# Norm sums as products with a matrix of ones, factors on all partitions, and pooling by doubling additions

## The chip, the cores and the metric

The kernel runs on one core of a Trainium2 chip. The metric is the device time of one execution in microseconds (us); the median of three runs of the kernel before is 1076.26 us (1076.07 to 1076.46).

## The reference

One decoder layer for two request groups that share all weights: one sequence of 256 new tokens, and 8 sequences with 4 new tokens each, 288 tokens in all. The model width is 2048; everything is fp32.

```python
h = rmsnorm(x, norm1_g)                                   # first norm
a, gate, z = split(h @ w_in + b_in, [1024, 1024, 1024])
u = a * sigmoid(gate)                                     # conv heads
c = silu(layernorm(depthwise_causal_conv(u_ext, conv_w, conv_b), ln_g, ln_b))
d = window_mean(z_ext, windows=(2, 4, 8, 16)) - z         # one window per 256 channels
p = grouped_matmul(d, pool_w) * pool_scale
x = x + concat([c, p]) @ w_out
f = square(relu(rmsnorm(x, norm2_g) @ w_ff1))             # 2048 -> 8192
x = x + f @ w_ff2
y = rmsnorm(x, norm_f)
```

`rmsnorm` needs for each token the sum of squares over 2048 channels; `layernorm` needs the mean and the sum of squares over 1024 channels. The window mean of the first tokens of a sequence divides by fewer elements than the window. The last inputs of the convolution and of the pooling are outputs too.

## The kernel before

Channels lie on the 128 partitions and the 288 tokens along the free axis, so that a [128 x 288] tile is one eighth of 1024 channels. Weights come from HBM as blocks of 512 KB (`wr`, 128 x 1024, six buffers). For fp32 accuracy each operand is split in a high part in fp32r and a low part, which is what the high part misses. `split` (L288) makes `whi` by an ACT copy (L293) and `wlo` by a subtraction (L294) on POOL or, for the second half of the w_out blocks, on DVE; each has four buffers. `product` (L297) is then three matmuls: high x high (L300), high x low (L301), low x high (L302). A `gemm` (L304) runs such products over the k-tiles for the two 128-column halves of a block pair, into two of four PSUM banks `ac`. After each gemm DVE evicts the banks.

The stages, in order: the first two groups of w_in columns on raw blocks (L367 to L400); five more conv groups and four pool groups in the order of `SEQUENCE`, with the small `pool_w` products (`mix_group`) between; the half of w_out that takes the pooled channels (eight gemms, loop at L548, operands `ph`, `pl`); the half that takes the convolved channels (L560, operands `mh`, `ml`); ff1 and ff2 in four chunks; the final norm. Matmuls of neighbouring gemms may be interleaved: a scheduler orders each engine's instructions from the program's priorities, and every engine then works through its own list strictly in that order. DVE also has a long low-priority list: the taps of the convolution (L443), and from ff1 on the products of some ff2 rows (`own_products`, L604).

What the change touches:

- **First norm.** `square` sums squares of x on all partitions into `tot` (L398). `token_sum` (L232) multiplies 96 tokens at a time by a column of ones, so that `total` is [96 x 3], tokens on partitions. `rsqrt_rows` (L266) takes ACT's square root, improves it with five small DVE instructions on [96 x 3] (L275 to L279), and spreads the factor over all partitions by three products with an identity into the bank `pr` (L285). DVE copies it to `rb` (L404), and every eviction of a w_in bank multiplies by `rb`.
- **LayerNorm of the convolution.** POOL adds up the eight tiles `c` in `sum_c`. `norm_begin` (L518), called after the third w_out gemm, multiplies `sum_c` by `avg`, a matrix of 1/1024 (L521, fp32), subtracts the mean from each tile (L524) and adds up squares in `ssc`. `norm_end` (L533), called after the fifth, does `token_sum` into `pt`, `rsqrt_rows` into `pr`, and for each tile: `n` = c times `pr` (DVE, L540), `cc` = Silu (ACT, L543), `mh` = copy (ACT, L544), `ml` = the rest (DVE, L545). `load_table` (L216) is an ACT instruction that brings in the table of the next function.
- **Pooling.** `pool_group` (L452) forms the window sum of a tile with `tensor_reduce` over a strided view (L471 for the sequence, L472 for the 8 x 4 sample tokens), for the window of 16 in two steps (L469 first). `rise` corrects the first tokens, and L474 and L476 divide by the window and subtract z. ACT copies to `dh` (L478), DVE makes `dl` (L479).

`column_sum` (L244) and `rsqrt_wide` (L249) already serve the norm ahead of ff1: two matmuls with a matrix of ones in fp32r put the sum on all partitions (`pss`, L247), and the same refinement runs on [128 x 288].

## Time and profile before

| | us |
|---|---|
| median of three runs | 1076.26 |
| the profiled execution | 1076.56 |
| its span | 1074.7 |
| PE busy | 1062.6 |
| DVE busy | 942.6 |
| POOL busy | 752.3 |
| ACT busy | 478.8 |

The span is the time from the first to the last instruction that the profiler saw; the profiled execution is 1.9 us longer than it. PE is TensorE, DVE VectorE, ACT ScalarE, POOL GpSimd and SP the engine that issues the DMAs; PEld is PE's loading of weights. PEclk is the share of TensorE's clock that was granted. A row such as `214.43 0.43 ACT L544 CAST mh<-cc` gives start, duration, engine, line, operation, and output and input by their names in the program. What stands behind the arrow in square brackets or after the bar is the idle time ahead of it and what ended it. An fp32 product (not fp32r) leaves two records.

### The profile page before, as it was taken

Reading aid. Unit: us, or ns where it says so; the run is one execution under the profiler, and the core shown is the slowest. Engines: PE = TensorE matmul, PEld = TensorE weight load, DVE = VectorE, ACT = ScalarE, POOL = GpSimd, SP = SyncE. Lnnn points to the kernel's source line nnn. Section 1 sums busy time; section 2 is a strip of 40 time slices with the busy share of each in tenths; the row PEclk is TensorE's granted clock in tenths of the full one; section 3 lists DMA queues with packets and bytes.
Section 4 is the critical chain, followed back from the end, with each engine's and each line's share of the span. In section 5 each row is a group of like instructions: output and inputs, shape, how many; then the busy total and the mean of one; then the engine's idle time right before and its main releaser. Section 6 shows DMA issues by size and latency. Waiting matters only on the chain.

```text
span 1074.7 us, 21425 instructions
## 1 busy us (share of the span) xinstructions
PE 1062.6 (99%) x8163; PEld 1061.3 (99%) x8163; DVE 942.6 (88%) x2117; ACT 478.8 (45%) x650; POOL 752.3 (70%) x400
## 2 busy tenths in 40 slices
PE   8999999999999999999999999999999999999996
PEld 8999999999999999999999999999999999999996
DVE  7799999687399999999999999999999999999553
ACT  7544455576445433334444333444433334444441
POOL 0899888503889987788888877888878788850001
PEclk9999999999999999999999999999999999999998
DMA  9655567565687777777797777777778888885522
GB/s 334 225 187 177 179 192 216 173 200 165 216 287 249 259 250 250 250 248 251 239 276 247 251 246 250 247 253 248 242 241 281 277 268 270 276 260 174 170 97 89
DMA packets 74663, 247.38 MB, mean 230 GB/s; under 512 B 7872, under 2 KB 17088, under 8 KB 74560
## 3 DMA queue, kind: packets, MB, share of 16 engines
q1 hardware_dynamic: 74128, 245.36, 70.0%
q8 instruction: 64, 1.05, 0.4%
q10 hardware_dynamic: 432, 0.64, 0.2%
q14 instruction: 39, 0.32, 0.1%
HBM read 241.25 MB, written 4.72 MB: 229 GB/s over the span
## 4 chain that ended last, share of the span: by engine, by line
PE 98%; DMA 0%; DVE 0%; ACT 0%; SPq 0%; issue 0%; DVEq 0%
PE ac L300 32%; PE ac L301 32%; PE ac L302 32%; PE ac L390 1%; PE cv L390 1%; DMA xT<-in_xT 0%; DVE xT L693 0%; PE pr L285 0%; ACT hh L376 0%; ACT uz L360 0%; PE pf L235 0%; ACT whi L383 0%; PE m L300 0%; PE m L302 0%; PE m L301 0%
## 5 line engine op out<-in xcount | busy, mean ns | idle before, releaser
L294 POOL TENSOR_TENSOR wlo<-wr,whi 128x1024 fp32r<-128x1024 f32 x282 | 675.7, 2404 | 177.9 <-ACT whi L293 177.1
L621 DVE SCALAR_TENSOR_TENSOR own<-uz,own 128x288 f32<-128x288 f32 x1397 | 605.1, 519 | 0.0
L293 ACT CAST whi<-wr 128x1024 fp32r<-128x1024 f32 x330 | 345.2, 1047 | 537.0 <-PE ac L301 485.1
L302 PE MATMUL ac<-ah,wlo 128*128 128x288 f32 x1024 | 298.1, 291 | 0.0
L301 PE MATMUL ac<-al,whi 128*128 128x288 f32 x1024 | 298.1, 291 | 0.0
L300 PE MATMUL ac<-ah,whi 128*128 128x288 f32 x1024 | 298.1, 291 | 0.0
L300 PE MATMUL ac<-fh,whi 128*128 128x288 f32 x1013 | 295.0, 291 | 0.0
L302 PE MATMUL ac<-fh,wlo 128*128 128x288 f32 x1013 | 294.9, 291 | 0.0
L301 PE MATMUL ac<-fl,whi 128*128 128x288 f32 x1013 | 294.9, 291 | 0.0
L302 PEld LDWEIGHTS ac<-ah,wlo 128*128 128x128 f32 x1024 | 191.7, 187 | 0.0
L300 PEld LDWEIGHTS ac<-ah,whi 128*128 128x128 f32 x1024 | 191.7, 187 | 0.0
L301 PEld LDWEIGHTS ac<-al,whi 128*128 128x128 f32 x1024 | 191.7, 187 | 0.0
L300 PEld LDWEIGHTS ac<-fh,whi 128*128 128x128 f32 x1013 | 189.6, 187 | 0.0
L301 PEld LDWEIGHTS ac<-fl,whi 128*128 128x128 f32 x1013 | 189.6, 187 | 0.0
L302 PEld LDWEIGHTS ac<-fh,wlo 128*128 128x128 f32 x1013 | 189.6, 187 | 0.0
L443 DVE SCALAR_TENSOR_TENSOR pc<-uz,vec,pc 128x256 f32<-128x256 f32 x232 | 99.2, 485 | 5.3 <-ACT pc L432 3.5
L301 PE MATMUL ac<-hl,whi 128*128 128x288 f32 x320 | 92.1, 291 | 0.0
L300 PE MATMUL ac<-hh,whi 128*128 128x288 f32 x320 | 92.0, 291 | 0.0
L302 PE MATMUL ac<-hh,wlo 128*128 128x288 f32 x320 | 87.3, 291 | 0.0
L294 DVE TENSOR_TENSOR wlo<-wr,whi 128x1024 fp32r<-128x1024 f32 x48 | 58.7, 1224 | 29.9 <-ACT whi L293 29.8
L693 POOL TENSOR_TENSOR xT<-xT,rg 128x576 f32<-128x576 f32 x2 | 2.8, 1408 | 99.4 <-ACT rg L698 99.4
L648 POOL TENSOR_TENSOR fl<-f,fh 128x288 fp32r<-128x288 f32 x64 | 53.5, 836 | 15.3 <-ACT fh L647 15.3
(174 smaller groups left out, 1056.0 us busy)
## 6 DMA issues: line engine op xcount, KB each, us to landing
wr<-in_w SPq DMA_DIRECT2D x336, 512.0 KB, 4.6
uz<-fd SPq DMA_DIRECT2D x96, 576.0 KB, 5.8
uz<-in_w SPq DMA_DIRECT2D x24, 128.0 KB, 6.8
out_u_out<-uz SPq DMA_DIRECT2D x1, 1208.0 KB, 8.8
xT<-in_xT SPq DMA_DIRECT2D x2, 576.0 KB, 8.1
uz<-in_hist_c SPq DMA_DIRECT2D x1, 1088.0 KB, 12.0
wr<-in_w SPq DMA_DIRECT2D x4, 256.0 KB, 5.4
xT<-in_xT SPq DMA_DIRECT2D x3, 288.0 KB, 6.1
```

Source lines behind the costliest of these rows:

```text
L293: nc.scalar.copy(hi[:, a:b, :], raw[:, a:b, :])
L294: eng.tensor_tensor(lo[:, a:b, :], raw[:, a:b, :], hi[:, a:b, :].bitcast(F32), op=ALU.subtract)
L300: nc.tensor.matmul(b, wh, xh, start=first, stop=False)
L301: nc.tensor.matmul(b, wh, xl, start=False, stop=False)
L302: nc.tensor.matmul(b, wl, xh, start=False, stop=last)
L390: nc.tensor.matmul(first_banks[m][:, :T], lhs(w, k, m), pair[k][x], start=c == 0 and k == 0 and w is hi and x == 0, stop=c == 7 and k == 1 ...
L443: nc.vector.scalar_tensor_tensor(out=dst, in0=u_all[:, i, w : w + SEQ], scalar=cw[i][:, w : w + 1], in1=pc[i], op0=ALU.mult, op1=ALU.add)
L621: nc.vector.scalar_tensor_tensor(out=to, in0=at[:, r, :], scalar=by, in1=to, op0=ALU.mult, op1=ALU.add)
L648: nc.gpsimd.tensor_tensor(fl, f, f32(fh), op=ALU.subtract)
L693: eng.tensor_tensor(xk, xk, by[:, None, :T].to_broadcast([P, n, T]), op=ALU.mult)
```

## The change

The first norm and the LayerNorm take `column_sum` and `rsqrt_wide` in place of `token_sum` and `rsqrt_rows`: `total` and `pt` become full banks, each filled by two fp32r products; their factors are computed on [128 x 288] and are on all partitions at once, so that the `pr` products and the copy to `rb` go. The mean is a column sum too, with the division put into the instruction that subtracts it. To split a row in `th` and `tl` an ACT copy and a DVE subtraction are added (`parts`; ff1's norm keeps POOL for both). Pooling adds shifted copies, with shift 1, 2, 4, 8: each step is an ACT copy of the running sum to PSUM and one DVE addition of that copy and the shifted sum. Lines of the new kernel stand 4 to 6 further down than in the old one.

```diff
+PAD = 32
...
+    gap = const.tile([P, PAD], F32, name="gap")
+    nc.gpsimd.memset(gap, 0.0)
...
-    avg = const.tile([P, P], F32, name="avg")
-    nc.vector.memset(avg, 1.0 / DC)
...
-    def parts(t):
+    def parts(t, hi=nc.scalar.copy, lo=nc.vector):
 
         th, tl = (tmpp.tile([P, T], F32R, name=nm(n), tag="tmp", bufs=6) for n in ("th", "tl"))
-        nc.gpsimd.tensor_copy(th, t)
-        nc.gpsimd.tensor_tensor(tl, t, f32(th), op=ALU.subtract)
+        hi(th, t)
+        lo.tensor_tensor(tl, t, f32(th), op=ALU.subtract)
         return th, tl
...
-    def rsqrt_wide(bank, out, scale):
+    def rsqrt_wide(bank, out, scale, after=None):
...
         nc.scalar.activation(s1, b, AF.Sqrt, bias=eps[:, 0:1], scale=scale)
+        if after is not None:
+            load_table(after, s1[:, 0:1])
...
-    total = ms("total", 8)
+    total = ms("total")
...
-                    token_sum(total, rows[0])
+                    column_sum(total, ones_r, hilo)
...
                     nc.vector.tensor_tensor(rows[0], squares[:, 0, 0], squares[:, 0, 1], op=ALU.add)
+                    hilo = parts(rows[0])
...
-    nc.vector.tensor_copy(rb, rsqrt_rows(total, 1.0 / D, AF.Sigmoid)[:, :T])
+    rsqrt_wide(total, rb, 1.0 / D, AF.Sigmoid)
...
-            b = ms("d")[:, :T]
-            s, step, n = z, 1, w
-            if w > 8:
-                s, step, n = tmp("s", ZL, "s", 2), 4, w // 4
-                nc.vector.tensor_reduce(s[:, 3:ZL], windows(z[:, 0 : ZL - 3], (1, ZL - 3), (1, 4)), axis=AX.X, op=ALU.add)
-            at = PH - step * (n - 1)
-            nc.vector.tensor_reduce(b[:, 0:SEQ], windows(s[:, at:], (1, SEQ), (step, n)), axis=AX.X, op=ALU.add)
-            nc.vector.tensor_reduce(samples(b[:, SEQ:T], NS), windows(s[:, ZO + at :], (ZS, NB), (1, NS), (step, n)), axis=AX.X, op=ALU.add)
+            s, r = ms("d"), z
+            for step in WINDOWS[: g + 1]:
+                n = ZL - step + 1
+                nc.scalar.copy(s[:, 0:n], r[:, 0:n])
+                to = s if step == w else tmp("r", ZL, "r", 2)
+                nc.vector.tensor_tensor(to[:, 0:n], s[:, 0:n], r[:, step // 2 : step // 2 + n], op=ALU.add)
+                r = to
+            at = PH - (w - 1)
...
-        nc.tensor.matmul(pmean[:, :T], avg, sum_c, start=True, stop=True)
+        column_sum(pmean, ones_r, parts(sum_c))
...
-            nc.vector.tensor_tensor(cs[i], cs[i], pmean[:, :T], op=ALU.subtract)
+            nc.vector.scalar_tensor_tensor(out=cs[i], in0=pmean[:, :T], scalar=-1.0 / DC, in1=cs[i], op0=ALU.mult, op1=ALU.add)
...
-        pt = ms("pt", 8)
-        token_sum(pt, ssc)
-        rl = rsqrt_rows(pt, 1.0 / DC, AF.Silu)
+        rl = ms("pt")
+        column_sum(rl, ones_r, parts(ssc))
+        rsqrt_wide(rl, rl[:, :T], 1.0 / DC, AF.Silu)
...
-    ss2 = parts(ss2)
+    ss2 = parts(ss2, nc.gpsimd.tensor_copy, nc.gpsimd)
```

The scheduler also orders three places anew. The first two are the LayerNorm, late in the pooled half of w_out. This is DVE's list there before (`wlo68`, `wlo69` are low parts of weights, `ac41` to `ac43` banks of the pooled half, `pt1` the sum, `st2` the factor's small tile, `pr2` the spread factor):

```order
L275 TENSOR_SCALAR pt1_2661<-pt1_2661 96x3
L276 RECIPROCAL st2_2665<-st2_2665 96x3
L277 TENSOR_TENSOR pt1_2661<-pt1_2661,st2_2665 96x3
L552 TENSOR_TENSOR xT_88<-xT_88,ac41_2804 128x288
L278 SCALAR_TENSOR_TENSOR st2_2665<-st2_2665,pt1_2661 96x3
L552 TENSOR_TENSOR xT_88<-xT_88,ac42_2805 128x288
L279 RECIPROCAL st2_2665<-st2_2665 96x3
L294 TENSOR_TENSOR wlo68_2927<-wr68_2920,whi68_2926 128x1024
L540 TENSOR_TENSOR n1_2677<-c1_540,pr2_2673 128x288
L294 TENSOR_TENSOR wlo69_2987<-wr69_2982,whi69_2986 128x1024
L540 TENSOR_TENSOR n2_2685<-c2_543,pr2_2673 128x288
L545 TENSOR_TENSOR ml1_2680<-cc1_2681,mh1_2679 128x288
```

And after (`s3`, `s4` are the wide temporaries, and the factor ends up in `pt1` itself):

```order
L258 TENSOR_SCALAR pt1_2697<-pt1_2697 128x288
L259 RECIPROCAL s4_2705<-s3_2704 128x288
L298 TENSOR_TENSOR wlo69_3023<-wr69_3018,whi69_3022 128x1024
L260 TENSOR_TENSOR pt1_2697<-pt1_2697,s4_2705 128x288
L558 TENSOR_TENSOR xT_88<-xT_88,ac43_2904 128x288
L558 TENSOR_TENSOR xT_88<-xT_88,ac44_2905 128x288
L261 SCALAR_TENSOR_TENSOR s4_2705<-s3_2704,pt1_2697 128x288
L298 TENSOR_TENSOR wlo70_3027<-wr70_3020,whi70_3026 128x1024
L262 RECIPROCAL pt1_2697<-s4_2705 128x288
L546 TENSOR_TENSOR n1_2713<-c1_539,pt1_2697 128x288
L546 TENSOR_TENSOR n2_2721<-c2_542,pt1_2697 128x288
```

Between the start of the factor and the first `n` one weight split and two evictions (`ac41`, `ac42`) stood before. Now two weight splits stand there and the evictions of `ac43` and `ac44`, the banks of the last pooled gemm. PE's list moved with it: before, the three `pt` products stood ahead of 34 matmuls of the pooled half, then the three `pr` products, and then 23 matmuls until the first `mh`; now the second `pt` product has 32 matmuls behind it, the last of the pooled half, and then comes `mh1`.

ACT's list at the same place before:

```order
L272 ACTIVATE st2_2665<-pt1_2661,eps_125 96x3
L218 ACT_TABLE_LOAD
L218 ACTIVATE few_124<-st2_2665 96x1
L293 CAST whi68_2926<-wr68_2920 128x1024
L293 CAST whi69_2986<-wr69_2982 128x1024
L543 ACTIVATE cc1_2681<-n1_2677,vec_87 128x288
L544 CAST mh1_2679<-cc1_2681 128x288
```

And after:

```order
L242 CAST th3_2698<-ssc1_2538 128x288
L297 CAST whi68_2962<-wr68_2956 128x1024
L255 ACTIVATE s3_2704<-pt1_2697,eps_125 128x288
L220 ACT_TABLE_LOAD
L220 ACTIVATE few_124<-s3_2704 128x1
L297 CAST whi69_3022<-wr69_3018 128x1024
L297 CAST whi70_3026<-wr70_3020 128x1024
L549 ACTIVATE cc1_2717<-n1_2713,vec_87 128x288
L549 ACTIVATE cc2_2725<-n2_2721,vec_87 128x288
L550 CAST mh1_2715<-cc1_2717 128x288
```

`whi69` and `whi70` both stand ahead of the first Silu now, and the second Silu ahead of the first copy `mh1`.

The third place is PE in the conv groups, at the seam of two gemms. Before, with the last reader of `whi25` 28 rows above the first row shown here:

```order
L300 MATMUL ac12_1282<-hh9_331,whi27_1191 128x288
L301 MATMUL ac12_1282<-hl9_332,whi27_1191 128x288
L300 MATMUL ac13_1447<-hh1_178,whi29_1383 128x288
L301 MATMUL ac13_1447<-hl1_179,whi29_1383 128x288
L300 MATMUL ac14_1448<-hh1_178,whi29_1383 128x288
```

And after:

```order
L304 MATMUL ac12_1281<-hh4_234,whi25_1178 128x288
L305 MATMUL ac12_1281<-hl4_235,whi25_1178 128x288
L306 MATMUL ac12_1281<-hh4_234,wlo25_1179 128x288
L304 MATMUL ac11_1280<-hh5_255,whi26_1182 128x288
L305 MATMUL ac11_1280<-hl5_256,whi26_1182 128x288
L304 MATMUL ac12_1281<-hh5_255,whi26_1182 128x288
L305 MATMUL ac12_1281<-hl5_256,whi26_1182 128x288
L304 MATMUL ac13_1446<-hh1_178,whi29_1382 128x288
```

`whi29` takes the buffer of `whi25` (four buffers, in turn). Its first product came 30 matmuls behind the last reader of that buffer, and now comes 6 behind.

## The prediction

> **What bounds the kernel now.** I read the chain that ended last first, then the waits of PE.

> ```profile
> PE 98%; DMA 0%; DVE 0%; ACT 0%; SPq 0%; issue 0%; DVEq 0%
> ```
> ```profile
> core 0 of [0], span 1074.7 us
> PE ac L390 <- ACT whi L383: 1.7, 1, 1.7
> PE warm L223 <- DVE ones L207: 1.1, 1, 1.1
> PE pr L285 <- DVE st L279: 0.5, 1, 0.5
> ```

> The chain is PE for 98% of the span, and these three waits are all that PE has; two fall in the first 9 us and one in the final norm. So PE issues without a stop, and only two things can move the time: fewer PE cycles, or a new PE wait. Work on DVE, ACT or POOL counts only where PE would wait for it. A change of 0.2% (2.15 us, hence 1074.1 to 1078.4) is about what a measurement here can tell from none.

> **PE's products.** The rows of PE's timeline at the sum `pt`, the spread `pr`, the mean `pmean`, and the products that will take their place (`pss`, in ff1's norm), with the groups of the like products of the first norm:

> ```profile
> L285 PE MATMUL pr<-ident,st 96*128 96x96 f32 x18 | 2.5, 274 | 0.5 <-DVE st L279 0.5
> L235 PE MATMUL total<-ones,tot 128*96 128x1 f32 x6 | 0.6, 214 | 0.0
> ```
> ```profile
> 207.47 0.59 PE L235 MATMUL pt<-ones,ssc 128*96 128x1 f32 x6
> 207.92 0.38 PE L300 MATMUL ac<-ph,whi 128*128 128x288 f32 x1
> 208.14 0.30 PE L301 MATMUL ac<-pl,whi 128*128 128x288 f32 x1
> ...
> 212.43 0.80 PE L285 MATMUL pr<-ident,st 96*128 96x96 f32 x6
> 213.02 0.38 PE L301 MATMUL ac<-pl,whi 128*128 128x288 f32 x1
> 213.23 0.29 PE L302 MATMUL ac<-ph,wlo 128*128 128x288 f32 x1
> ```
> ```profile
> 196.58 0.65 PE L521 MATMUL pmean<-sum_c,avg 128*128 128x288 f32 x2
> 196.85 0.51 PE L301 MATMUL ac<-pl,whi 128*128 128x288 f32 x1
> 197.20 0.29 PE L302 MATMUL ac<-ph,wlo 128*128 128x288 f32 x1
> ```
> ```profile
> 276.67 0.30 PE L247 MATMUL pss<-tl,ones_r 128*128 128x288 f32 x1
> 276.81 0.29 PE L302 MATMUL ac<-ah,wlo 128*128 128x288 f32 x1
> ```

> Matmuls overlap, so starts are subtracted, not durations added. Ordinary matmuls start 0.13 apart (156 in 20 us in the row of windows under Pooling). From `pt` at 207.47 to the second matmul behind it at 208.14 is 0.67; less one regular 0.13 the sum costs 0.54. `pr` costs 213.23 - 212.43 - 0.13 = 0.67. `pmean` costs 197.20 - 196.58 - 0.13 = 0.49. The first norm's `total` has the same six records of the same mean length, and its `pr` is among the 18 records of one mean, so 0.54 and 0.67 again. Removed: 2 x 0.54 + 2 x 0.67 + 0.49 = 2.91 us. Added: six fp32r products that cost 276.81 - 276.67 = 0.14 each, 0.84. **Net -2.07 us**, sure as far as PE goes.

> **First norm.** The factor now needs the wide chain (rows below): from the second `total` product 0.3 + 0.5 + 0.37 + 1.94 + 0.9 + 2.0 = 6 us, some 3 us more than the small one. PE works meanwhile on the third conv group in the two free `ac` banks, 96 matmuls or 12.5 us long, and `rb` is first needed by the evictions that free banks for the group after. Cost taken: nothing; if the cover were too short, at most those 3 us.

> **Pooling.** The grouped rows of the reductions, and PE, DVE and ACT in the busiest stretch:

> ```profile
> L471 DVE TENSOR_REDUCE d<-uz 128x256 f32<-128x2048 f32 (+2 forms) x6 | 8.4, 1406 | 0.0
> L469 DVE TENSOR_REDUCE s<-uz 128x420 f32<-128x1680 f32 x2 | 3.8, 1894 | 0.0
> L471 DVE TENSOR_REDUCE d<-s 128x256 f32<-128x1024 f32 x2 | 3.8, 1888 | 0.0
> ```
> ```profile
> 120.00:140.00 20.00, 20.00 (x156) 20.00 (x155) 20.00 (x51) 11.02 (x20) 14.39 (x7) 1.00 0.59 187
> ```

> The last row gives busy us of PE, PEld, DVE, ACT and POOL. DVE is full there, yet PE does not wait: it is filled with low-priority taps. The change takes 16 us of reductions (and the small sample ones) from DVE and gives it 2 x (1 + 2 + 3 + 4) = 20 additions of some 422 columns. A 288-column DVE instruction has a pitch of 0.37 (rows below), so an estimate of 0.37 x 422 / 288 = 0.54 each, 11 us: DVE gains 5 us or more, off PE's path. ACT, 11 of 20 busy, gets 20 copies; from the 0.43 of the `mh` copy an estimate of 0.63 each, 12.6 us. Per tile the chain becomes longer for all windows: for 16, 4 x (0.63 + 0.54) = 4.7 where L469 and L471 took 3.8. The queues that matter are ACT's: behind these copies, each of which waits for DVE, stand casts of weights that PE will need. Bounds: 0 (PE's operands still early; no gain is possible where PE does not wait) to 1 us; I take **+0.3**, since the chain grows by about a microsecond per tile and PE has a whole gemm between a pool group and its mix.

> A side effect of the new order is nearer to PE: `whi29` is used 6 matmuls behind the last reader of its buffer. The reader starts at 0 and ends after 0.29; the cast takes 1.05 (the `whi` row below); PE arrives after 6 x 0.13 = 0.78. 1.34 + 0.03 - 0.78 = **+0.6**; between 0.4 and 0.9.

> SP's queue has ff2's eight loads for `turned` two weight blocks earlier; those blocks are read a whole gemm later. Nothing.

> **The LayerNorm decides.** First the wide chain as it runs in ff1's norm, where it has cover, on DVE and on ACT:

> ```profile
> 278.64 0.47 DVE L254 TENSOR_SCALAR pss<-pss 128x288 f32<-128x288 f32 x1 [3.05 <-ACT s L253]
> 279.01 1.94 DVE L255 RECIPROCAL s<-s 128x288 f32<-128x288 f32 x1
> ...
> 281.98 1.95 DVE L258 RECIPROCAL r<-s 128x288 f32<-128x288 f32 x1
> ```
> ```profile
> 278.10 0.50 ACT L253 ACTIVATE s<-pss,eps 128x288 f32<-128x288 f32 x1
> ```

> Then the place itself in the kernel before, ACT, DVE and PE:

> ```profile
> 208.37 1.28 ACT L218 ACT_TABLE_LOAD   x1
> 209.67 0.20 ACT L218 ACTIVATE few<-st 96x1 f32<-96x1 f32 x1
> ...
> 212.42 1.05 ACT L293 CAST whi<-wr 128x1024 fp32r<-128x1024 f32 x1 [1.61 <-issue]
> 213.77 0.63 ACT L543 ACTIVATE cc<-n,vec 128x288 f32<-128x288 f32 x1 [0.30 <-DVE n L540]
> 214.43 0.43 ACT L544 CAST mh<-cc 128x288 fp32r<-128x288 f32 x1
> ```
> ```profile
> 213.28 0.46 DVE L540 TENSOR_TENSOR n<-c,pr 128x288 f32<-128x288 f32 x1 [1.21 <-PE pr L285]
> 213.65 1.22 DVE L294 TENSOR_TENSOR wlo<-wr,whi 128x1024 fp32r<-128x1024 f32 x1
> 214.78 0.45 DVE L540 TENSOR_TENSOR n<-c,pr 128x288 f32<-128x288 f32 x1
> 215.15 0.46 DVE L545 TENSOR_TENSOR ml<-cc,mh 128x288 fp32r<-128x288 f32 x1
> ```
> ```profile
> 216.09 0.42 PE L300 MATMUL ac<-mh,whi 128*128 128x288 f32 x2
> ```

> Before, `mh` is ready at 214.43 + 0.43 = 214.86 and PE arrives at 216.09: 1.2 us to spare, with 8.6 us of matmuls between `pt` and `mh`. After, the order leaves 32 matmuls behind the second `pt` product: with it 0.14 + 32 x 0.13 = 4.3 us, and PE's next instruction needs `mh1`. From that product's start: it ends at 0.30; ACT's root from 0.34 to 0.84. ACT then loads the table (1.28), does `few` (0.2) and casts `whi69` (1.05): 3.4. DVE meanwhile does L254 (pitch 279.01 - 278.64 = 0.37) and the reciprocal (1.94): 3.2. Then its list runs in order: `wlo69` (pitch 214.78 - 213.65 = 1.13) from 3.4 to 4.5; L256, two evictions and L257 at 0.37 each (pitch 215.15 - 214.78), to 6.0; `wlo70` 1.13, to 7.1; the second reciprocal 1.95 + 0.1, to 9.2; `n1` until the Silu may start, 213.77 - 213.28 = 0.49, to 9.7; two Silu of about 0.6, to 10.9; `mh1` 0.43, to 11.3. PE is free at 4.3: a **wait of 7.0 us**. Bounds: 6.5 (Silus pipelined, hand-overs free) to 7.8 (each of some eight hand-overs 0.1 dearer). After it, a k-step (n, Silu, copy, rest) takes under 1.1 us of ACT and 0.74 of DVE, PE's 12 matmuls for it in four banks 1.56: no further wait.

> **The clock after the wait.** The kernel's end, PE's last row and the windows behind it (PEclk is the third number from the end):

> ```profile
> 1065.26 0.83 PE L285 MATMUL again<-ident,st 96*128 96x96 f32 x6
> ```
> ```profile
> 1066.00:1068.00 2.00, 0.09 (x1) 0.00 (x0) 2.00 (x4) 0.40 (x1) 1.40 (x2) 1.00 0.51 183
> 1069.00:1070.00 1.00, 0.00 (x0) 0.00 (x0) 0.53 (x1) 0.00 (x0) 0.38 (x1) 0.65 1.05 414
> ```

> PE ends at 1066.09. The mean clock of 1069 to 1070 is 0.65, which is 0.3 us at 1 and the rest at 0.5: the clock halved at 1069.3, 3.2 us after the last matmul. The 1.7 us wait near the start is shorter than that; 7 us is longer. So PE resumes at half clock. How long, no row of before shows. If the rise takes as long as the fall, 3.2 us give 1.6 us' worth of work: **+1.6**. Bounds 0 to 3.2.

> [...]

> **Sum.** -2.07 + 0.3 + 0.6 + 7.0 + 1.6 = +7.4 on the profiled 1076.56, or 1084.0; that execution lies 0.3 above the median of the runs, so against the median 1076.26 + 7.4 = **1083.7 us**.

> **Rivals.**
> - *The wait is covered, only PE's saving is left.* If the chain from the `pt` product to `mh1` took no more than 4.3 us, the time would be 1076.26 - 2.07 = 1074.2, and with `whi29` covered too as much. It decides at 4.3 us. Two reciprocals of 1.95 and the root alone take 4.4, so the rows speak against it; for it speaks only that the records do not show every dependence. 0.1, half of it below 1074.1.
> - *The wait without the clock.* 1083.7 - 1.6 = 1082.1. [...] 0.25.
> - *ACT is late in the pool stage too.* DVE is full, and ACT's 11 of 20 us get 12.6 us of copies over some 45 us on top: if a copy waits behind a weight cast in each of the 20 steps for half its 1.05, the chains of a group's two tiles lag by 4 x 0.5 = 2 us or more and PE loses some 3 us: 1086.7. Against it: PE has a whole gemm there. 0.1.
> - *Half of the wait goes*, because evictions or casts run earlier than the list suggests: 1079 to 1080. 0.05.

> The forecast keeps 0.5. Range 1080.0 to 1086.0: the forecast and the case without the clock with their bounds; the covered case, most of the late pool stage and the halved wait are left out. Faster by over 0.2%: 0.06; within 0.2%: 0.08; slower: 0.86.

> **What would show it.** PE's list of waits should have a new entry for `mh`, released by ACT, of 6.5 to 7.8 us near 216, and one of 0.4 to 0.9 for `whi29`; PEclk should dip to 0.5 in the windows behind the first. Two `pt` records of 0.3 should stand where six stood, and `pr` only at the end. No wait for `mh` would make the forecast wrong, as would waits for `dh` or `whi` in the pool stage of more than 1 us.

## The result, and the profile after

The changed kernel takes 1083.75 us (median of 4 runs, 1083.05 to 1084.36) against 1076.16 of the kernel before in the same comparison: a ratio of 1.0070, 95% interval 1.0053 to 1.0088. It is slower by 7.6 us. The profiled execution took 1084.13 us, its span is 1082.2, the mean granted clock 0.994 (0.997 before).

PE's list of waits, all of it (line, released by, us in total, times, longest):

```profile
PE ac L304 <- ACT mh L550: 6.6, 1, 6.6
PE ac L394 <- ACT whi L387: 1.2, 1, 1.2
PE warm L225 <- DVE ones L211: 1.1, 1, 1.1
PE ac L304 <- ACT whi L297: 0.5, 1, 0.5
PE pr L289 <- DVE st L283: 0.4, 1, 0.4
```

Two entries are new, the first and the fourth. The chain that ended last now leads through DVE and ACT:

```profile
PE 97%; DVE 1%; ACT 1%; DMA 0%; issue 0%; SPq 0%; DVEq 0%; ACTq 0%
```

PE's timeline from the second `pt` product to the clock's return:

```profile
210.47 0.29 PE L249 MATMUL pt<-tl,ones_r 128*128 128x288 f32 x1
...
214.64 0.29 PE L306 MATMUL ac<-ph,wlo 128*128 128x288 f32 x1
221.52 1.33 PE L304 MATMUL ac<-mh,whi 128*128 128x288 f32 x4 [6.59 <-ACT mh L550]
222.64 0.44 PE L305 MATMUL ac<-ml,whi 128*128 128x288 f32 x1
...
226.24 0.33 PE L306 MATMUL ac<-mh,wlo 128*128 128x288 f32 x1
...
226.54 0.29 PE L306 MATMUL ac<-mh,wlo 128*128 128x288 f32 x1
```

The last product of the pooled half starts at 214.64, and the next could have at 214.77; it starts at 221.52, 6.75 us later. Then the matmuls come 0.24 apart and not 0.13, until 226.3. What DVE and ACT did meanwhile:

```profile
211.34 0.47 DVE L258 TENSOR_SCALAR pt<-pt 128x288 f32<-128x288 f32 x1 [0.70 <-ACT s L255]
211.71 1.94 DVE L259 RECIPROCAL s<-s 128x288 f32<-128x288 f32 x1
213.79 1.23 DVE L298 TENSOR_TENSOR wlo<-wr,whi 128x1024 fp32r<-128x1024 f32 x1
214.93 0.46 DVE L260 TENSOR_TENSOR pt<-pt,s 128x288 f32<-128x288 f32 x1
215.30 0.81 DVE L558 TENSOR_TENSOR xT<-xT,ac 128x288 f32<-128x288 f32 x2
216.02 0.45 DVE L261 SCALAR_TENSOR_TENSOR s<-s,pt 128x288 f32<-128x288 f32 x1
216.39 1.22 DVE L298 TENSOR_TENSOR wlo<-wr,whi 128x1024 fp32r<-128x1024 f32 x1
217.52 1.95 DVE L262 RECIPROCAL pt<-s 128x288 f32<-128x288 f32 x1
219.51 1.60 DVE L546 TENSOR_TENSOR n<-c,pt 128x288 f32<-128x288 f32 x4
```
```profile
210.81 0.50 ACT L255 ACTIVATE s<-pt,eps 128x288 f32<-128x288 f32 x1 [1.43 <-PE pt L249]
...
212.73 1.03 ACT L297 CAST whi<-wr 128x1024 fp32r<-128x1024 f32 x1
...
220.00 1.14 ACT L549 ACTIVATE cc<-n,vec 128x288 f32<-128x288 f32 x2 [4.12 <-DVE n L546]
221.05 0.41 ACT L550 CAST mh<-cc 128x288 fp32r<-128x288 f32 x1
```

DVE works almost without a pause from 211.34 on; of its 8.2 us up to the first `n`, 3.9 are the two reciprocals, 1.1 the factor's three short instructions, 2.3 the two weight splits and 0.7 the two evictions that stand in its list. The windows with the clock (third number from the end):

```profile
219.00:219.50 0.50, 0.00 (x0) 0.00 (x0) 0.48 (x1) 0.00 (x0) 0.00 (x0) 0.99 0.87 287
219.50:220.00 0.50, 0.00 (x0) 0.00 (x0) 0.49 (x2) 0.00 (x0) 0.00 (x0) 0.50 0.94 360
...
224.00:226.00 2.00, 2.00 (x10) 2.00 (x9) 1.62 (x5) 2.00 (x6) 0.00 (x0) 0.50 0.00 0
226.00:226.50 0.50, 0.50 (x4) 0.50 (x4) 0.23 (x1) 0.50 (x3) 0.00 (x0) 0.68 0.00 0
226.50:227.00 0.50, 0.50 (x6) 0.50 (x5) 0.38 (x2) 0.42 (x2) 0.00 (x0) 1.00 0.00 0
```

The clock is halved at 219.5 and back at 226.3 (0.68 is 0.32 us at a half and 0.18 at one). The trace's record of the clock gives 6.83 us.

To see where the 7.6 us arise I numbered the ordinary matmuls in both traces (8079 in each) and subtracted the starts of the same number, each from the first. Just ahead of the first norm's product the difference is under 0.1. It falls by 0.94 at the first norm, rises by 0.80 at the seam of `whi29`, falls by 0.2 at the mean and by 0.95 at the LayerNorm's products, rises by 6.75 at `mh1` and by 2.26 over the next 20 matmuls, and does not move after that.

### The profile page after: what moved, and what is told of

It reads as the page before. It is cut to its first block, busy times and chain, and to the rows that moved or that the text cites. A ratio compares the mean times of both kernels' runs of the same rounds, so it can differ in the third digit from the quotient of the medians.

```text
span 1082.2 us, 21406 instructions
## 1 busy us (share of the span) xinstructions
PE 1063.5 (98%) x8143; PEld 1061.6 (98%) x8143; DVE 949.1 (88%) x2120; ACT 488.8 (45%) x673; POOL 752.6 (70%) x401
## 3 DMA queue, kind: packets, MB, share of 16 engines
q8 instruction: 64, 1.05, 0.4%
## 4 chain that ended last, share of the span: by engine, by line
PE 97%; DVE 1%; ACT 1%; DMA 0%; issue 0%; SPq 0%; DVEq 0%; ACTq 0%
PE ac L304 32%; PE ac L306 31%; PE ac L305 31%; PE ac L394 1%; PE cv L394 1%; DMA xT<-in_xT 0%; DVE xT L699 0%; DVE wlo L298 0%; ACT whi L297 0%; DVE pt L262 0%; ACT hh L380 0%; ACT uz L364 0%; ACT cc L549 0%; PE pf L237 0%; ACT whi L387 0%
```

## The experiments

Each experiment was timed beside the kernel before (medians 1076.2 to 1076.4). The theory is that of the prediction: the LayerNorm's wide factor has too few matmuls over it, PE waits, and the clock falls. The rivals put the loss in pooling, in the first norm, or in operands that come late behind the wait.

| run | us | ratio to before (95%) | PE waits for `mh`, `ml` | half clock |
|---|---|---|---|---|
| full change | 1083.75 | 1.0053 to 1.0088 | 6.6 | 6.83 |
| e1 LayerNorm by rows | 1077.37 | 1.0001 to 1.0018 | 0.6 | none |
| e2 LayerNorm alone | 1083.38 | 1.0052 to 1.0079 | 5.4 | 6.83 |
| e3 20 idle products | 1083.45 | 1.0053 to 1.0078 | 2.1 | 3.41 |
| e4 old pooling | 1086.53 | 1.0080 to 1.0107 | 9.2 | 10.24 |
| e5 first norm alone | 1078.48 | 1.0014 to 1.0033 | 1.7 | none |
| e6 pooling alone | 1076.08 | 0.9989 to 1.0007 | none | none |
| e7 28 idle products | 1081.76 | 1.0038 to 1.0063 | 0.3 | none |
| e8 splits on POOL | 1080.35 | 1.0026 to 1.0051 | 3.6 | 6.83 |
| e9 bare reciprocal | 1079.14 | 1.0014 to 1.0035 | 2.6 | 3.41 |
| e10 queues freed | 1079.74 | 1.0021 to 1.0045 | 3.3 | 6.83 |
| e11 all, queues freed | 1081.69 | 1.0039 to 1.0064 | 3.7 | 6.83 |
| e12 as e10, `cc` in PSUM | 1077.41 | 1.0004 to 1.0022 | 1.1 | none |

The last two columns are those of the profiled execution, in us. That execution need not be the median: in e10 it took 1081.85 us, in e8 1081.33.

**e1 and e2: the LayerNorm's factor taken out, and by itself.**

```diff
-        rl = ms("pt")
-        column_sum(rl, ones_r, parts(ssc))
-        rsqrt_wide(rl, rl[:, :T], 1.0 / DC, AF.Silu)
+        pt = ms("pt", 8)
+        token_sum(pt, ssc)
+        rl = rsqrt_rows(pt, 1.0 / DC, AF.Silu)
```

> The changed kernel with only the LayerNorm's factor put back to rows of tokens (token_sum, rsqrt_rows and the spread by identity); first norm, mean and pooling stay as changed. Theory (the wait for mh1 and the half clock behind it are the whole loss): both go, PE pays 0.95 us for the old products, so against the kernel before -2.09 + 0.95 + 0.80 for the seam at whi29 = -0.3 us, about 1075.8. Rival (the pool stage or the first norm costs several us): the time stays above 1078.

1077.37: the large wait and the half clock are gone, 6.4 us of the 7.6. But it is 1 us slower than before, not 0.3 faster:

```profile
PE ac L304 <- ACT mh L550: 0.4, 1, 0.4
PE ac L305 <- DVE ml L551: 0.2, 1, 0.2
```

By the numbered matmuls these waits and their restarts cost 1.4 us. The sum for e1 counted products only. In e1's order a weight split stands directly ahead of the first `n` on DVE (212.85 to 213.99), and a second Silu ahead of `mh1` on ACT, so that `mh1` is ready at 215.93 (214.86 before), while PE comes for it 0.5 us sooner than before. e2 is the reverse, the kernel before with the lines marked `-` above (and `parts` on ACT and DVE).

> The kernel before with only the LayerNorm's factor made wide (two column products and rsqrt_wide); first norm, mean and pooling stay as before. The order leaves 49 matmuls (6.5 us) behind the second pt product, and DVE's list holds three weight splits and two evictions inside the chain. Theory: from that product's start, root 0.84, first reciprocal done at 3.2, wlo68 1.1, L256 after it, wlo69 1.1, L257, eviction, second reciprocal, eviction, wlo70 1.1, n1, two Silu, mh1: 0.84 + 0.4 + 1.9 + 3 x 1.13 + 4 x 0.37 + 2.05 + 0.5 + 1.1 + 0.4 = 12.1 at least; a wait of 5.5 us for mh1, 0 to 2.3 us of half clock, PE saves 0.95: 1080.7 to 1083. Rival (without the pooling or the first norm the wide factor is covered): 1075.2.

1083.38, 0.4 above the upper end: the wait is 5.4 us for the 5.5 that were expected, and the half clock lasted 6.83 and cost 2.4 by the numbered matmuls. The wide factor alone makes nearly the whole loss.

**e3 and e7: PE kept at work in the wait**, by 20 and by 28 products that nothing reads.

```diff
+    idle = bank("idle", cvp, "cv")
+    for _ in range(20):
+        nc.tensor.matmul(idle[:, 0:P], ones, ones, start=True, stop=True)
```

> The changed kernel with 20 idle fp32 products of 128 columns (ones by ones, into a bank that nothing reads) put on PE between the pooled half of w_out and the first mh1 product; about 5.5 us at full clock, so that they end before mh1 is there. Theory (2.26 us of the loss are the half clock behind the wait): the wait as seen from the real products stays near 6.75, but the clock stays at 1 and the time falls by 2.0 to 2.3, to about 1081.6. Rival (the 0.24 pitch behind the wait is operands that come late, not the clock): the time stays at 1083.7.

1083.45: missed. PE's timeline and the windows show why:

```profile
214.64 4.63 PE L565 MATMUL idle<-ones 128*128 128x128 f32 x40
221.39 0.79 PE L304 MATMUL ac<-mh,whi 128*128 128x288 f32 x4 [2.12 <-ACT mh L550]
```
```profile
221.00:222.00 1.00, 0.61 (x4) 0.61 (x5) 0.56 (x2) 1.00 (x4) 0.00 (x0) 1.00 0.00 0
222.00:223.00 1.00, 1.00 (x7) 1.00 (x6) 0.97 (x3) 1.00 (x4) 0.00 (x0) 0.61 0.00 0
...
225.00:226.00 1.00, 1.00 (x7) 1.00 (x7) 0.65 (x2) 1.00 (x3) 0.00 (x0) 0.68 0.00 0
```

The products took 4.63 us and not 5.5. They ended at 219.27, so PE was idle for 2.1 us only, and the clock still fell, at 222.2, when PE was already at work again, until 225.6. The slow stretch is 3.41 us and not 6.83, and cost 1.7 us by the numbered matmuls instead of 2.26. So e3 did not keep the clock up; e7 does.

> As the run with 20 idle products, but 28 of them: 6.5 us at the 0.23 each took there, from 214.8 to 221.2, so that PE is idle for a few tenths only before mh1 comes. Theory (the half clock follows from a window of 3.4 us in which PE was mostly idle): no window is idle now, the clock stays at 1, PE's pitch behind the wait is 0.13, and the time is 2.2 less than that of the full change: about 1081.4. Rival (the slow pitch is operands that come late): 1083.5.

1081.76, 2.0 below the full change:

```profile
214.82 6.41 PE L565 MATMUL idle<-ones 128*128 128x128 f32 x56
221.57 0.79 PE L304 MATMUL ac<-mh,whi 128*128 128x288 f32 x4 [0.34 <-ACT mh L550]
222.20 0.29 PE L305 MATMUL ac<-ml,whi 128*128 128x288 f32 x1
222.33 0.29 PE L306 MATMUL ac<-mh,wlo 128*128 128x288 f32 x1
```

`mh1` comes as late as before, but the pitch behind it is 0.13 and the clock stays at 1. The slow pitch was the clock, not late operands. e7 is also the rival of the prediction that has the wait without the clock, which it put at 1082.1.

**e4 and e6: pooling put back, and pooling alone.** In e4 the loop of copies and additions gives way to the three `tensor_reduce` of before; e6 is the reverse.

```diff
-            for step in WINDOWS[: g + 1]:
...
-                nc.scalar.copy(s[:, 0:n], r[:, 0:n])
...
-                nc.vector.tensor_tensor(to[:, 0:n], s[:, 0:n], r[:, step // 2 : step // 2 + n], op=ALU.add)
+            nc.vector.tensor_reduce(b[:, 0:SEQ], windows(s[:, at:], (1, SEQ), (step, n)), axis=AX.X, op=ALU.add)
```

> The changed kernel with pooling put back to tensor_reduce; the three norm sums stay as changed. The order now puts both pt products behind the last matmul of the pooled half. Theory (the doubling additions give DVE time, which the LayerNorm uses): nothing covers the wide chain, so PE waits 8 to 10 us and the half clock costs 2 more; 1085 to 1087, slower than the full change. Rival (the doubling additions, with their 20 copies on ACT, are part of the loss): faster than the full change, below 1083.

1086.53, a wait of 9.2 us for `mh` and three stretches of 3.41 us at half clock. The doubling additions are not part of the loss; without them it is 2.8 us larger.

> The kernel before with only the pooling changed to doubling additions. Theory: no product is saved and PE has no wait for dh, dl or whi in the pool stage (the prediction took 0.3 us for one); DVE ends its taps earlier, and the mean's product stands 25 rows earlier than before: the time is that of before, 1076.3 +- 0.4. Rival (the 20 copies hold up ACT's weight casts): 1077 or more with a wait for whi or dh between 120 and 170 us.

1076.08, the time of before within the interval, with no wait for `whi` or `dh` in the pool stage. What they give is time on DVE, whose last tap of the convolution ends 4.7 us earlier (187.92, before 192.58), and before had no use for it.

**e5: the first norm alone.**

> The kernel before with only the first norm changed (two column products and the wide chain); LayerNorm, mean and pooling as before. The prediction took the 3 us by which rb comes later at nothing. If that holds: PE saves 0.94, the seam at whi29 costs 0.80, 1076.2. Rival: rb's delay is passed on through DVE's list to the last convolution taps, the mean and the LayerNorm; the order has the pt products 33 rows later than before and the spread two rows ahead of mh1, so PE waits there 2 to 2.5 us, and perhaps for a window of half clock: 1078 to 1080.

1078.48, in the rival's range. The factor `rb` is ready 2.7 us later (DVE's first eviction that uses it starts at 34.09 before and at 36.79 here). The last addition into `sum_c` on POOL, before and then in e5:

```profile
193.03 0.81 POOL L448 TENSOR_TENSOR sum_c<-sum_c,c 128x288 f32<-128x288 f32 x1
```
```profile
193.37 2.39 POOL L296 TENSOR_TENSOR wlo<-wr,whi 128x1024 fp32r<-128x1024 f32 x1 [0.72 <-ACT whi L295]
195.71 0.81 POOL L451 TENSOR_TENSOR sum_c<-sum_c,c 128x288 f32<-128x288 f32 x1
```

2.7 us later, 160 us downstream; `pt` then came at 211.60 (207.47 before) and PE waited 1.7 us for `mh`. Only 0.5 us of this comes straight through DVE, whose last tap ends at 193.05 (192.58 before). The rest is POOL's list, in which a weight split (the first row) now stands directly ahead of the last addition. So the rival's way, through DVE's list alone, is only a part. That the scheduler moved the split because of the later `rb` is likely, but no run shows it. In the full change the time that the pooling gives DVE pays for the delay: the last tap ends at 190.33 and the same addition stands at 192.83 there.

**e8 and e9: the chain made shorter.** e8 makes four of the low weight parts on POOL; e9 leaves the refinement of the root out.

```diff
-        for _ in range(8):
-            yield halves([split(raw, V) for raw in load()])
+        for j in range(8):
+            yield halves([split(raw, G if j < 2 else V) for raw in load()])
```

> The changed kernel with the low parts of the first four weight blocks of the convolved half of w_out (wlo67 to wlo70) made by POOL, which is idle there, and no longer by DVE. The order leaves 38 matmuls (5.1 us) behind the second pt product, and no weight split in DVE's chain. Theory: from that product root 0.84, first reciprocal at 3.2, L256, L257, second reciprocal to 6.2, two evictions 0.74, n1 0.5, two Silu 1.1, mh1 0.4, in all 9.0: a wait of 3.9 us, down from 6.75, and one or two windows of half clock (1.5 to 2.2): 1080.3 to 1081.1. Rival (the wide chain itself, not what stands in its queue, is the wait): 1083.

1080.35, with a wait of 3.6 us for the 3.9 worked out from the two lists. From the second `pt` product to `mh1`'s first product it is 8.8 us and not 11.05: 2.3 us of the wait were the two weight splits that stood between the factor's instructions, and 0.8 are six more matmuls of cover in the new order.

```diff
-        rsqrt_wide(rl, rl[:, :T], 1.0 / DC, AF.Silu)
+        s1 = tmp("s")
+        nc.scalar.activation(s1, rl[:, :T], AF.Sqrt, bias=eps[:, 0:1], scale=1.0 / DC)
+        load_table(AF.Silu, s1[:, 0:1])
+        nc.vector.reciprocal(rl[:, :T], s1)
```

> The changed kernel whose LayerNorm factor is the bare reciprocal of ACT's root; the refinement (three short DVE instructions and the second reciprocal, 3 us of the chain) is left out. Theory: root 0.84, reciprocal to 2.8, wlo69 to 4.5, n1 at 5.0, but ACT casts whi70 only when PE has left the buffer, to 5.4, then two Silu and mh1, to 7.1; 4.3 us are covered: a wait of 2.8 us in place of 6.75, and none or one window of half clock (0 or 1.6): 1077.8 or 1079.4. Rival (the refinement's length does not matter, the queue does): above 1081.

1079.14 (1077.72 to 1079.68), wait 2.6, one stretch of half clock in the profiled execution: the second of the two cases.

**e10, e11, e12: cover for the wide factor.** All three free the LayerNorm's queues (the last addition into `sum_c` and the weight splits of its place change engine); e10 and e12 have the first norm by rows, e11 has it as changed.

```diff
-                else:
+                elif i < N8 - 1:
                     nc.gpsimd.tensor_tensor(sum_c, sum_c, cs[i], op=ALU.add)
+                else:
+                    nc.vector.tensor_tensor(sum_c, sum_c, cs[i], op=ALU.add)
...
-            yield halves([split(raw, V) for raw in load()])
+            yield halves([split(raw, G if j < 2 else V, hi_by=nc.gpsimd.tensor_copy if j == 1 else nc.scalar.copy) for raw in load()])
```

> The changed kernel with the first norm put back to rows, and three moves that free the LayerNorm's queues: the last addition into sum_c on DVE, the low parts wlo67 to wlo70 on POOL, and whi69 and whi70 on POOL. The order leaves 60 matmuls (7.9 us) behind the second pt product, DVE's chain has two evictions and no split, ACT's one cast. Theory: chain to mh1 8.6, a wait of 0.7 us, no half clock; PE saves 0.93 for the LayerNorm and 0.21 for the mean: 1075.8, 0.4 below the kernel before. Rival (the wide factor cannot be covered in this place): above 1077.

1079.74: missed, though the reason was right as far as it went. The waits of e10:

```profile
PE ac L305 <- DVE ml L552: 2.9, 3, 1.5
PE ac L304 <- ACT mh L551: 0.4, 1, 0.4
```

`mh1` is in time to 0.4 us, so the wide factor is covered there. The loss is a new wait, for `ml`, and half clock behind it. The profiled execution is the longest of six; the three shortest took 1078.8 to 1079.2, still 3 us above the forecast. On DVE, and on POOL beside it:

```profile
215.72 0.52 DVE L552 TENSOR_TENSOR ml<-cc,mh 128x288 fp32r<-128x288 f32 x1
...
216.52 2.26 DVE L552 TENSOR_TENSOR ml<-cc,mh 128x288 fp32r<-128x288 f32 x1
218.71 0.81 DVE L547 TENSOR_TENSOR n<-c,pt 128x288 f32<-128x288 f32 x2
219.43 1.89 DVE L552 TENSOR_TENSOR ml<-cc,mh 128x288 fp32r<-128x288 f32 x1
```
```profile
215.89 5.12 POOL L298 TENSOR_TENSOR wlo<-wr,whi 128x1024 fp32r<-128x1024 f32 x2
```

While POOL makes its two splits, `ml`, which reads `cc` and `mh` from SBUF, takes 2.26 and 1.89 us and not 0.45, and each ends 0.3 us after a split (at 218.47 and 221.00); `n`, whose factor lies in PSUM, keeps its 0.44 (216.16 to 216.60). One difference between the two is that `n` has only one input in SBUF; e12 gives `ml` the same.

> The full change with the same three moves (last addition into sum_c on DVE, wlo67 to wlo70 and whi69, whi70 on POOL). The order leaves 54 matmuls (7.2 us) behind the second pt product, but DVE evicts a bank of the last pooled gemm ahead of n1, which PE ends shortly before: n1, Silu and mh1 follow it, 1.8 us of wait. Theory: -2.09 for the products, 0.80 for the seam at whi29, 1.8 for the wait, no half clock: 1076.8. Rival (a loss elsewhere in the change): above 1079.

1081.69: missed for the same reason, with waits of 1.6 us for `mh` and 2.1 for `ml`.

> The run with the LayerNorm's queues freed (first norm by rows, last addition into sum_c on DVE, wlo67 to wlo70, whi69 and whi70 on POOL), with one more move: the Silu's result cc lies in PSUM for seven of eight tiles, so that DVE's subtraction for ml has only one operand in SBUF. In that run ml took 2.26 and 1.89 us instead of 0.45 and ended when a split on POOL ended. Theory (an fp32 subtraction on DVE with all operands in SBUF waits while POOL works, one with an operand in PSUM does not): every ml takes 0.45 to 0.55 although POOL makes wlo69 and wlo70 beside it; the order puts ml1 behind two evictions and two more products on DVE, 1 to 1.5 us of wait; no half clock: 1076.3 to 1077. Rival (ml was long for another reason, such as its wait for mh): some ml still take about 2 us and the time stays near 1079.7.

In e12 `cc` lies in PSUM (`bank("cc", cvp, "cv")` in place of `tmp("cc")`). 1077.41, and the same place on DVE, with POOL's splits from 215.72 to 220.43:

```profile
216.09 0.81 DVE L547 TENSOR_TENSOR n<-c,pt 128x288 f32<-128x288 f32 x2
216.82 0.81 DVE L552 TENSOR_TENSOR ml<-cc,mh 128x288 fp32r<-128x288 f32 x2
218.93 0.82 DVE L552 TENSOR_TENSOR ml<-cc,mh 128x288 fp32r<-128x288 f32 x2 [1.30 <-ACT mh L551]
```

Every `ml` has its 0.45 again, as expected, and the profiled execution has no half clock. The time is 0.4 above the range that was expected. No version that I ran beats the kernel before; the nearest is e6, which is equal to it.

## Why the prediction was right

The forecast was 1083.7 and the measurement 1083.75, by these terms:

| step | forecast | measured |
|---|---|---|
| PE's products | -2.07 | -2.1 |
| pool stage | +0.3 | 0 (e6) |
| seam at `whi29` | +0.6 | +0.8 |
| wait for `mh1` | +7.0 | +6.75 |
| half clock | +1.6 | +2.26 |
| sum | +7.4 | +7.7 by the numbered matmuls, +7.6 by the medians |

That the forecast is met to 0.05 us is partly luck: the pool stage and the wait came out 0.55 below their terms, the seam and the clock 0.86 above, and these misses nearly cancel. The range is not the sum of the bounds either; they add up to 1081.1 to 1087.1, and 1080.0 to 1086.0 was stated.

- **The products** came out to a tenth.
- **The wait** followed from the order of DVE's and ACT's lists with durations from rows of before; each stop on the way (`wlo69` first, then two evictions, `wlo70`, the second Silu ahead of `mh1`) is in the rows after. The two Silu took 1.14 rather than 1.2, and the hand-overs from one engine to the next took 0.03 to 0.06 us by the rows. e8 and e9, worked out in the same manner, met 3.6 and 2.6 us for 3.9 and 2.8.
- **The half clock** had the right cause (e7) and too small a size. The step that failed is "3.2 us after the last matmul" and as much for the rise: the fall came 4.6 us after the last matmul ended, and the rise 4.8 us after PE resumed, so that PE worked 4.8 us at half pace. Both changes lie on the grid of 3.41 us that the last section describes. At the end of the kernel before, PE stopped 0.2 us behind a line of that grid; here it stopped 1.15 us ahead of one. The prediction also says that no row of before shows how long a rise takes. The start of before does: the first products, `warm`, start 0.21 us apart until 4.2 and 0.11 apart from 4.4 on, so that full pace came 3.3 us after the first of them.
- **`whi29`**: the mechanism holds, with 0.1 more in the hand-overs and 0.1 in the first matmuls behind the wait:

```profile
85.89 0.29 PE L305 MATMUL ac<-hl,whi 128*128 128x288 f32 x1
86.71 0.40 PE L304 MATMUL ac<-hh,whi 128*128 128x288 f32 x1 [0.53 <-ACT whi L297]
```
```profile
85.61 1.05 ACT L297 CAST whi<-wr 128x1024 fp32r<-128x1024 f32 x1 [1.15 <-POOL wlo L298]
```

  The last reader of the buffer starts at 85.24 and ends at 85.53, the cast runs from 85.61 to 86.66, PE goes on at 86.71. The row names POOL as the releaser, whose split ended at 85.55. In all nine runs with this order the cast starts 0.08 us behind the reader's end, while the last split on POOL ends up to 2.6 us earlier in some of them, so it waits for PE.
- **The first norm at nothing** was wrong by its reason. The cover named there, the third conv group, does protect PE at that place, but the order that goes with the later `rb` brings the LayerNorm's sum 2.7 us later, and PE waits 1.7 us there (e5). The total was not touched, because the pooling's gift to DVE (e4, e6), which the prediction called off PE's path, stands at the same place with the other sign; the order that the wait was worked out from had both in it.
- **A covered wait** (the rival below before) needed a chain under 4.3 us; measured it is 11.05, from 210.47 to 221.52.

What stays open: how much of e5's new order on POOL follows from the later `rb`, and whether the first norm's 0.94 us can be had without the seam at `whi29` was not tried.

## What to carry to other kernels

Where PE is always busy, as here, a sum moved to all partitions saves PE products (2.1 us in this kernel) but turns a [96 x 3] chain into a [128 x 288] one (11.05 us from the second `pt` product to `mh1`'s); count the matmuls that stand between the sum and its first use in the new order before counting the products saved. A chain on an engine that works through its list in order is as long as everything that the list holds between its links (3.0 of DVE's 8.2 us were splits and evictions), so read the list, not the chain. Work that has cover where it stands can still cost at the next tight place: a factor 2.7 us late at 34 us went with a sum 2.7 us late at 196, 0.5 of it through DVE and the rest through a new place in POOL's list.

## What the runs showed of the hardware

```profile
L243 DVE TENSOR_TENSOR tl<-sum_c,th 128x288 fp32r<-128x288 f32 x1 | 2.2, 2215 | 3.8 <-ACT th L242 3.8
L243 DVE TENSOR_TENSOR tl<-ssc,th 128x288 fp32r<-128x288 f32 x1 | 0.5, 452 | 0.0
```
